# Attention's value product in groups of four query tiles, in a hybrid encoder block

## The chip, the cores and the metric

The kernel runs on one core of one Trainium2 chip. The metric is the device time of one execution in microseconds (us), as the median of several runs. Before the change that is 3035.97 us over 3 runs, from 3034.92 to 3040.51.

## The reference

One encoder block over 2048 positions of width 1024, all in f32. Cut to what matters here:

```python
proj = rms_norm(h, ln_mix_g) @ w_in                  # one combined input projection
y_a  = mlstm_group(...)                              # 4 heads x 128, chunks of 128, both directions
# y_b: 4 heads of attention over all 2048 keys
sc = einsum('bqhd,bkhd->bhqk', q_nope, k_nope) + einsum('bqhr,bkr->bhqk', q_rope, k_rope)
pr = softmax(sc * scale, axis=-1)
y_b = einsum('bhqk,bkhd->bqhd', pr, v)
h = h + concatenate([y_a, y_b], -1) @ w_out
h = h + conv_gated_mlp(rms_norm(h, ln_ffn_g), ...)   # up 1024 -> 2 x 2816, conv of 3, gate, down
h = h + sigmoid(rms_norm(h, ple_norm_g) @ w_ple_gate) * rms_norm(p @ w_ple_proj, ple_post_g)
out = rms_norm(h, final_g)
```

## The kernel before

All large products are made three times: each f32 operand is split into a high and a low part (`split`: ScalarE casts the high part, L114, VectorE subtracts to get the low one, L117), and `mm3` (L125) multiplies low by high, high by low and high by high into the same PSUM bank. The stages follow each other: `in_proj`, `attend` with the mLSTM as side work, `out_proj`, `up`, `down` with the last part, `ple`. Buffers in SBUF are places with fixed names: x0 to x15, w0 to w13, t0 to t7, s0 to s2 and u0 to u2; who writes a place waits for its last readers. Instructions of an engine stand in one order, which a scheduler makes at build time from the order in the source; in the last part of `in_proj` PE's order is the written one. Tiles named in a profile row stand without their numbers (pt, pe, bk).

**In the input projection** the columns "rest" (gates, latent queries, keys and rope part) come first. `turn_rest` (L273) transposes each 128 rows into PSUM, copies them to `rt` in place t6 (L278) and stores them (L279). The query and key columns of the mLSTM come last, 8 blocks of 128 columns (L376), while the side work `absorb`, `gates` and `q_up` is pumped.

**Attention** (`attend`, L827) makes 64 rounds, head after head, one per query tile of 128 rows. Keys and values are the same latent for all heads. A round is written as a list of steps:

```python
order = "s0 E1 . s1 E2 . . t0 . s2 . E3 . t1 . s3 . . X e0 t2 . . t3 V . .".split()
```

- s0 to s3 (`score_bank`, L846): the next tile's scores against 512 keys each, five products into one of four PSUM banks, then the row maximum on VectorE (L857).
- X (`soft`, L866): the maximum over the four banks and its scaling (L868, L869, tile nm).
- e0, and E1 to E3 in the following round (`expo`, L872): the exponentials from PSUM into pe on ScalarE with their row sums (L875). A score bank is free for the tile after once its exponential has been read. E3 is followed by the reciprocal of the row sum, into `rsums`.
- t0 to t3 (`transp`, L883): four transposes each of the current tile's probabilities into PSUM (L889, tile tb) and a split into pt, which holds two query tiles, 256 columns.
- V (`pv`, L892): half of the product of the values with pt of two query tiles, 24 matmuls of 256 columns into one bank (ppv); both halves take two rounds, so that every round has one. After the second, the reciprocals are transposed to rows (L908), copied (L910), multiplied onto the product (L911) and stored in `y_d`.
- each dot lets `pump` take some 0.73 steps of the side work, the mLSTM (L689), whose matmuls share one PSUM bank (ml, tile mb).

Tile 0's scores, maxima and exponentials come ahead of the first round (L931 to L939), behind the projection's last block.

**The output projection** (`out_proj`, L1031) loads y for 128 rows (`load_y`, L1012), splits it, multiplies it by w_out (eight splits `wo`, in x0 to x7, four of them made within attention), adds x, stores h1 and normalises (`norm_load`, L981; the scaling is L987). The last tile's transposes come at the head of `up` (`turn`, L1274). `sums` (L1109) makes differences of blocks of the normalised rows and stores them in `t_d`; `load_op` (L1129) loads and splits them for `up`. `down` (L1351) loads its weights as it goes (`load_w`, L1369).

Of the kernel before, what the change touches and what calls it, by code (L numbers as in the profile page):

```python
# [18 lines left out]
P = 128  # L19
# [17 lines left out]
SIDE = 610  # L37
# [22 lines left out]
class Block:  # L60
# [4 lines left out]
    def __init__(self, ctx, tc, d):  # L65
# [20 lines left out]
        self.vv_d = dt([P, NT, P], F32, name="vv_d")  # L86
        self.wo_d = dt([NH, P, D], F32, name="wo_d")
# [90 lines left out]
    def in_proj(self):  # L178
# [94 lines left out]
        def turn_rest(st, nn):  # L273
            pt = self.ppv.tile([P, 4, P], F32, name="rtp", tag="pv")
            for j in range(4):
                nc.tensor.transpose(pt[:, j, :], nn[:, j * P:(j + 1) * P], self.ident)
            rt = self.at("t6", [P, 4, P], name="rt")
            nc.scalar.copy(rt, pt)  # L278
            nc.sync.dma_start(self.rest_d[:, :, st * P:(st + 1) * P], rt)  # L279
# [59 lines left out]
        side, due = chain(self.absorb(), self.gates(), self.q_up()), 0.0  # L339
# [16 lines left out]
        def pump(due):  # L356
            due += 1.17
            while due >= 1:
                next(side, None)
                due -= 1  # L360
            return due

        def conv(j, u, c):
            t = self.at(next(trot), [P, 512], name="ct")
            uu, o = u[c // 2], (c % 2) * 512
# [7 lines left out]

        with self.tc.manual_schedule(engines={mybir.EngineType.PE}):
            nxt = load_qk(0)
            for j in range(8):  # L376
                ws = nxt
                if j < 7:
                    nxt = load_qk(j + 1)
                else:  # L380
                    kr = self.load_kr()
                    kv = [self.load_kv(i, w) for i, w in enumerate(("w8", "w13", "w9", "w12"))]
                u = [self.at(next(urot), [P, H + 2], name="u") for _ in range(2)]
                nc.vector.memset(u[0][:, 0:1], 0.0)
                nc.vector.memset(u[1][:, H + 1:H + 2], 0.0)
                order = range(4) if j < 7 else (3, 2, 1, 0)
                for c in order:
                    ps = self.bank()
                    for kt in range(KT):
                        f, k = divmod(kt, 4)  # L390
                        self.mm3(ps, ws[f][:, k, 0], ws[f][:, k, 1], xh[c][f][:, k, :], xl[c][f][:, k, :],
                                 kt == 0, kt == KT - 1)
                        if kt % 2 and kt < KT - 1:
                            due = pump(due)
                    o = (c % 2) * 512
                    nc.vector.tensor_tensor(u[c // 2][:, 1 + o:513 + o], ps, rrow[c // 2][:, o:o + 512], op=ALU.mult)
                    if c == 1:
                        nc.vector.tensor_copy(u[1][:, 0:1], u[0][:, H:H + 1])
                    if c == 2:
                        nc.vector.tensor_copy(u[0][:, H + 1:H + 2], u[1][:, 1:2])  # L400
                    due = pump(due)
                    if c != order[0] and (j < 7 or c > 0):
                        conv(j, u, c - 1 if j < 7 else c + 1)
                    if j == 7 and c == 3:
                        self.split_kr(kr)
                    if j == 7 and c == 2:
                        for _ in self.split_kv(kv, range(2)):
                            pass
                if j < 7:
                    conv(j, u, 3)  # L410
        for _ in side:
            pass

        def tail():
            for c in (1, 0):
                conv(7, u, c)
                yield
            yield from pause(4)
            yield from self.split_kv(kv, range(2, 4))
# [30 lines left out]
    def split_kv(self, raws, quarters):  # L450
        for i in quarters:
# [8 lines left out]
            for e in range(2):  # L460
                sl = slice((i % 2) * 1024 + e * 512, (i % 2) * 1024 + e * 512 + 512)
                self.split(raws[i][:, e * 512:e * 512 + 512], hi[:, sl], lo[:, sl])
                yield
# [225 lines left out]
    def mlstm(self):  # L689
# [38 lines left out]
        for c in range(NT - 1, 0, -1):  # L728
            kT = self.at(f"w{5 + c % 2}", [P, NH, P], name="kTb")
            nc.sync.dma_start(kT, self.qk_d[c, :, 4:8, :])  # L730
            v1 = load_v(c)
# [95 lines left out]
    def attend(self, side):  # L827
        nc = self.nc
        mm = nc.tensor.matmul
        prot, ptrot = _rot("w", (0, 1, 2)), _rot("x", (8, 9, 4, 5, 6, 7))  # L830
        kh, kl, qv = self.kh, self.kl, {}
        self.wo = []
# [39 lines left out]
        def expo(s, kb):  # L872
# [5 lines left out]
            if kb == 3:  # L878
                ri = rsums[:, s.h * NT + s.qt:s.h * NT + s.qt + 1]
                nc.vector.tensor_reduce(ri, s.rs, axis=AX.X, op=ALU.add)  # L880
                nc.vector.reciprocal(ri, ri)

        def transp(s, kb, pts):  # L883
# [6 lines left out]
            self.split(t, pts[kb][:, 0, :, o:o + P], pts[kb][:, 1, :, o:o + P])  # L890

        def pv(w, half):  # L892
            h, pr, pts = w.h, w.pr, w.pts
            if half == 0:
                w.ps = self.ppv.tile([P, 256], F32, name="ppv", tag="pv")
            vh, vl = self.vh, self.vl
            for kb in (2 * half, 2 * half + 1):
                for j in range(4):
                    kt = kb * 4 + j
                    ks = slice(kt * P, (kt + 1) * P)  # L900
                    self.mm3(w.ps, vh[:, ks], vl[:, ks], pts[kb][:, 0, j, :], pts[kb][:, 1, j, :],
                             kt == 0, kt == NT - 1)
            if half == 1:

                pb = self.tbank([P, 2, P])
                for i in range(2):
                    k = h * NT + 2 * pr + i
                    nc.tensor.transpose(pb[:, i, :], rsums[:, k:k + 1].broadcast_to([P, P]), self.ident)  # L908
                rb = self.at(f"s{pr % 3}", [P, 2, P], name="ya")
                nc.scalar.copy(rb, pb)  # L910
                nc.vector.tensor_tensor(rb, rb, w.ps.rearrange("p (a t) -> p a t", a=2), op=ALU.mult)  # L911
                for i in range(2):
                    nc.sync.dma_start(self.y_d[2 * pr + i, :, 4 + h, :], rb[:, i])
# [4 lines left out]
        order = "s0 E1 . s1 E2 . . t0 . s2 . E3 . t1 . s3 . . X e0 t2 . . t3 V . .".split()  # L918
        first = [o for o in order if o[0] == 'e']
        rate = SIDE / (len(seq) * order.count("."))  # L920
# [10 lines left out]
        load_q(0, 0)  # L931
        split_q(0, 0)
        load_q(0, 1)
        cur = start(*seq[0])
        for kb in range(4):
            score_bank(cur, kb)
        soft(cur)
        for o in first:
            expo(cur, int(o[1]))  # L939
        pts, pend = [], None  # L940
        for i, (h, qt) in enumerate(seq):
            if h == NH - 1 and qt in (4, 6, 8, 10):
                self.load_wo(qt // 2 - 2)
# [7 lines left out]
            if nxt is None:  # L951
                self.ps0 = self.pml.tile([P, 512], F32, name="wo0", tag="ml")
                self.out_mm(self.ps0, self.y0, range(4), slice(0, 512))
            for op in order:
# [10 lines left out]
                elif op[0] == "E":  # L965
                    expo(cur, int(op[1]))
                elif op == "V" and qt % 2:
                    pend = Tile()
                    pend.h, pend.pr, pend.pts = h, qt // 2, pts
                    pv(pend, 0)  # L970
                elif op == "V" and pend is not None:
                    pv(pend, 1)
            if qt % 2:
                pts = []
            cur = nxt
        pv(pend, 1)
# [27 lines left out]
    def load_wo(self, k):  # L1004
        nc = self.nc
        raw = self.at("w13" if k < 4 else ("w13", "w12")[k % 2], [P, D], name="wor")
# [24 lines left out]
    def out_proj(self):  # L1031
# [7 lines left out]
        for k in range(4, KT):  # L1039
# [4 lines left out]
        self.orot = _rot("t", (4, 5)), _rot("t", range(6))  # L1044
        sums, b11 = self.sums(0), self.load_op(0, "B11")
        for c in range(NT):
# [6 lines left out]
            if 9 <= c < 13:  # L1053
                next(sums)
                next(b11)
            if c in (13, 14):
                for _ in self.load_op(0, f"T{c - 12}"):
                    pass
# [5 lines left out]
            for hf in range(2):  # L1064
# [3 lines left out]
                self.out_mm(ps, y, range(4 if begun else 0, KT), fs)  # L1068
# [40 lines left out]
    def sums(self, b):  # L1109

        nc = self.nc
        t0 = b * 2 * SB
        for k in range(4):
# [6 lines left out]
            tt = nc.vector.tensor_tensor  # L1120
            tt(b12, b12, b11, op=ALU.subtract)
            tt(b22, b22, b12, op=ALU.subtract)
            tt(b11, b22, b11, op=ALU.subtract)
            tt(b21, b21, b22, op=ALU.subtract)
            for i, t in enumerate((b12, b22, b11, b21)):
                nc.sync.dma_start(self.t_d[b, i, :, k], t)
            yield

    def load_op(self, b, n):  # L1129

        hi, lo = [self.at(f"x{x}", [P, 4, SB], F32R, f"op{e}") for x, e in zip(self.OPX[n], "hl")]
        if b:
            self.xop[n] = hi, lo
        else:
            self.__dict__.setdefault("xop", {})[n] = hi, lo
        rot = self.orot[b or n != "B11"]
# [414 lines left out]
```

## Time and profile before

| what | value |
|---|---|
| median of 3 runs | 3035.97 us |
| the profiled execution's own time | 3039.24 us |
| its span, first to last instruction | 3037.5 us |
| mean granted clock of TensorE | 0.996 |
| PE busy | 2979.3 us, 98% |
| VectorE (DVE) busy | 1891.2 us, 62% |
| ScalarE (ACT) busy | 1358.1 us, 45% |
| DMA | 431.06 MB, mean 142 GB/s |

How to read it: the page has shares of busy time, then groups of instructions: source line, engine, operation, tile written <- tiles read, shape, count, then busy us and mean ns of one, then the idle time of the engine just ahead of them and what ended most of it. In the timeline a row has the start in us, the time it took, the engine and line, and in brackets the idle time of its engine ahead of it with what ended that. Matmuls are pipelined: the time between two starts is shorter than the duration of one, and a PE that is busy need not be at its peak. A window's row has its length, then the busy time and count of each engine, the granted clock, and the DMA's share and rate.

### The profile page before, as it was taken

Reading aid. Unit: us, or ns where it says so; the run is one execution under the profiler, and the core shown is the slowest. Engines: PE = TensorE matmul, PEld = TensorE weight load, DVE = VectorE, ACT = ScalarE, POOL = GpSimd, SP = SyncE. Lnnn points to the kernel's source line nnn. Section 1 sums busy time; section 2 is a strip of 40 time slices with the busy share of each in tenths; the row PEclk is TensorE's granted clock in tenths of the full one; section 3 lists DMA queues with packets and bytes.
Section 4 is the critical chain, followed back from the end, with each engine's and each line's share of the span. In section 5 each row is a group of like instructions: output and inputs, shape, how many; then the busy total and the mean of one; then the engine's idle time right before and its main releaser. Section 6 shows DMA issues by size and latency. Waiting matters only on the chain. (4 is left out here: it accounts for less than half of the span.)

```text
span 3037.5 us, 40758 instructions
## 1 busy us (share of the span) xinstructions
PE 2979.3 (98%) x15184; PEld 2517.3 (83%) x15184; DVE 1891.2 (62%) x3457; ACT 1358.1 (45%) x2598; POOL 141.5 (5%) x262
## 2 busy tenths in 40 slices
PE   8999999999999999999999999999999999999998
PEld 7888788888898898888778887788887888888887
DVE  7321756777777777635788888777777343334565
ACT  7211545555566565523544445444444332223444
POOL 3100000000000000000000000000000000000111
PEclk9999999999999999999999999999999999999999
DMA  6522446443333232558764335433337465444221
GB/s 190 112 70 91 124 124 190 126 146 104 101 96 93 93 98 97 171 187 303 228 210 139 132 134 198 139 125 125 124 122 229 160 221 200 146 159 148 78 79 63
DMA packets 323383, 431.06 MB, mean 142 GB/s; under 512 B 24992, under 2 KB 218480, under 8 KB 323184
## 3 DMA queue, kind: packets, MB, share of 16 engines
q1 hardware_dynamic: 323184, 428.46, 43.6%
q8 instruction: 119, 1.95, 0.3%
q14 instruction: 80, 0.66, 0.1%
HBM read 291.12 MB, written 137.26 MB: 141 GB/s over the span
## 5 line engine op out<-in xcount | busy, mean ns | idle before, releaser
L127 PE MATMUL facc<-fw,hid 128*128 128x512 f32 x2112 | 480.7, 389 | 3.9 <-ACT fw L114 2.7
L127 PEld LDWEIGHTS facc<-fw,hid 128*128 128x128 f32 x2112 | 396.2, 188 | 87.7 <-ACT fw L114 3.1
L127 PE MATMUL fxy<-oph,fw 128*128 128x512 f32 x1408 | 451.7, 394 | 6.4 <-DVE ug L1307 5.0
L127 PEld LDWEIGHTS fxy<-oph,fw 128*128 128x128 f32 x1408 | 265.7, 189 | 75.8 <-DVE ug L1307 11.5
L117 DVE TENSOR_TENSOR fw<-fwr,fw 128x1024 fp32r<-128x1024 f32 x176 | 215.3, 1223 | 165.1 <-ACT fw L114 165.1
L114 ACT CAST fw<-fwr 128x1024 fp32r<-128x1024 f32 x176 | 184.4, 1048 | 256.0 <-PE facc L127 131.6
L127 PE MATMUL fxy<-opl,fw 128*128 128x512 f32 x704 | 276.1, 392 | 0.0
L114 ACT CAST pt<-tb 128x512 fp32r<-128x512 f32 x256 | 146.9, 586 | 211.3 <-PE tb L889 210.4
L127 PE MATMUL bk<-wsp,xh 128*128 128x512 f32 (+1 forms) x768 | 235.6, 388 | 0.2 <-DVE wsp L123 0.2
L127 PE MATMUL fzs<-oph,fw 128*128 128x512 f32 x704 | 234.2, 389 | 0.0
L127 PE MATMUL ppv<-pt,kv 128*128 128x256 f32 x1536 | 203.7, 287 | 0.0
L117 DVE TENSOR_TENSOR pt<-tb,pt 128x512 fp32r<-128x512 f32 x256 | 174.0, 686 | 40.0 <-ACT pt L114 38.7
L857 DVE TENSOR_REDUCE mx<-bk 128x1 f32<-128x512 f32 x256 | 175.3, 685 | 35.8 <-PE bk L856 34.9
L127 PEld LDWEIGHTS ppv<-pt,kv 128*128 128x128 f32 x1536 | 188.9, 191 | 0.0
L875 ACT ACTIVATE pe<-bk,nm 128x512 f32<-128x512 f32 x256 | 173.9, 694 | 25.5 <-DVE nm L869 24.4
L127 PE MATMUL pgp<-pw,x3s 128*128 128x512 f32 (+1 forms) x792 | 178.7, 385 | 0.0
L127 PE MATMUL bk<-wo,yhl 128*128 128x512 f32 x744 | 174.4, 392 | 0.0
L127 PE MATMUL bk<-xh,wqk 128*128 128x512 f32 x512 | 168.1, 394 | 0.0
L127 PEld LDWEIGHTS pgp<-pw,x3s 128*128 128x128 f32 x792 | 144.5, 188 | 28.2
L127 PEld LDWEIGHTS bk<-wsp,xh 128*128 128x128 f32 x768 | 145.6, 190 | 26.5 <-DVE wsp L123 1.2
L127 PEld LDWEIGHTS bk<-wo,yhl 128*128 128x128 f32 x744 | 138.3, 188 | 28.2
L127 PE MATMUL bk<-wsp,xl 128*128 128x512 f32 (+1 forms) x384 | 150.5, 392 | 7.7 <-ACT wsp L122 7.4
(317 smaller groups left out, 5374.6 us busy)
## 6 DMA issues: line engine op xcount, KB each, us to landing
fwr<-in_w_down SPq DMA_DIRECT2D x88, 512.0 KB, 4.0
fwr<-in_w_up SPq DMA_DIRECT2D x66, 512.0 KB, 4.1
s_d<-fwr SPq DMA_DIRECT2D x44, 512.0 KB, 3.2
fws<-s_d SPq DMA_DIRECT2D x44, 512.0 KB, 3.6
hraw<-hid_d SPq DMA_DIRECT2D x33, 512.0 KB, 4.2
rw<-row_d SPq DMA_DIRECT2D x32, 512.0 KB, 5.1
hid_d<-fgv SPq DMA_DIRECT2D x22, 512.0 KB, 3.7
hid_d<-fgv SPq DMA_DIRECT2D x22, 511.5 KB, 5.1
```

Source lines behind the costliest of these rows:

```text
L114: nc.scalar.copy(hi, src)
L117: (sub or nc.vector).tensor_tensor(lo, src, _f(hi), op=ALU.subtract)
L127: mm = lambda *a, **k: self.nc.tensor.matmul(*a, **k, skip_group_check=more)
L857: nc.vector.tensor_reduce(s.mx[:, kb:kb + 1], ps, axis=AX.X, op=ALU.max)
L875: nc.scalar.activation(s.pe[:, kb % 2], s.banks[kb], AF.Exp, bias=s.nm, scale=ASCALE, accum_out=s.rs[:, kb:kb + 1])
```

## The change

The probabilities of four query tiles now form one group: pt is two tiles of 512 columns (high and low), in ten places of which a group takes eight. The product has 512 columns and takes four steps V, one for each 512 keys: two in the round that ends a group (`fourth`) and two in the next (`after`); the two rounds between (`plain`) have none, and more dots. The reciprocals of the row sums are no longer transposed for each pair: they are turned once for half of the tiles, stored in `ri_d`, and `load_y` multiplies by them. Attention begins inside the projection (`attend_begin`): the scores, maxima and exponentials of tile 0 stand among the last four blocks of matmuls, two of which go to other PSUM banks. `rt` has two places. Two output weights, not four, are split within attention. The differences of `sums` are split straight from SBUF where they had been stored and loaded again, and two weights of `down` are loaded ahead of the last steps of `up`.

```diff
-            rt = self.at("t6", [P, 4, P], name="rt")
+            rt = self.at(f"u{st % 2}", [P, 4, P], name="rt")
...
-            due += 1.17
...
+            due[0] += 1.26
...
+            att = self.attend_begin()
+            next(att)
+            vals = [self.load_kv(2 + i, w) for i, w in enumerate(("w5", "w7"))]
+            block(6, 0, self.bank)
+            conv(6, 1)
+            conv(6, 0)
+            next(att)
+            block(7, 1, self.gbank)
+            conv(7, 2)
+            next(att)
+            block(7, 0, self.gbank)
+            conv(7, 1)
+            conv(7, 0)
...
+        ptrot = _rot("x", (8, 9, 4, 5, 6, 7, 0, 1, 2, 3))
+        lastrot = _rot("x", range(2, 10))
...
         def transp(s, kb, pts):
-            o = (s.qt % 2) * P
-            if s.qt % 2 == 0:
-                pts.append(self.at(next(ptrot), [P, 2, 4, 256], F32R, "pt"))
+            o = (s.qt % 4) * P
+            if o == 0:
+                rot = lastrot if s.h == NH - 1 and s.qt == NT - 4 else ptrot
+                pts.append([self.at(next(rot), [P, 4, 512], F32R, f"pt{e}") for e in "hl"])
             t = self.tbank()
             for j in range(4):
                 nc.tensor.transpose(t[:, j, :], s.p[kb][:, j * P:(j + 1) * P], self.ident)
-            self.split(t, pts[kb][:, 0, :, o:o + P], pts[kb][:, 1, :, o:o + P])
...
+            self.split(t, pts[kb][0][:, :, o:o + P], pts[kb][1][:, :, o:o + P])
+
+        def pv(w):
+
+            kb = w.kb
+            w.kb += 1
+            if kb == 0:
+                w.ps = self.ppv.tile([P, 512], F32, name="ppv", tag="pv")
             vh, vl = self.vh, self.vl
-            for kb in (2 * half, 2 * half + 1):
...
+            for j in range(4):
+                kt = kb * 4 + j
+                ks = slice(kt * P, (kt + 1) * P)
+                self.mm3(w.ps, vh[:, ks], vl[:, ks], w.pts[kb][0][:, j, :], w.pts[kb][1][:, j, :], kt == 0, kt == NT - 1)
+            if kb == 3:
+                ya = self.at(f"u{w.g % 2}", [P, 4, P], name="ya")
+                nc.scalar.copy(ya, w.ps.rearrange("p (a t) -> p a t", a=4))
+                for i in range(4):
+                    nc.sync.dma_start(self.y_d[4 * w.g + i, :, 4 + w.h, :], ya[:, i])
...
-        order = "s0 E1 . s1 E2 . . t0 . s2 . E3 . t1 . s3 . . X e0 t2 . . t3 V . .".split()
...
+        plain = "s0 E1 . . s1 E2 . . . t0 . . s2 . E3 . . t1 . s3 . . X e0 . t2 . . t3 . .".split()
+        fourth = "s0 E1 . s1 E2 . t0 . s2 . E3 t1 V . s3 . X e0 t2 . V t3 .".split()
+        after = "s0 E1 . s1 E2 V t0 . s2 . E3 . t1 . s3 . X e0 V t2 . t3 .".split()
+        orders = after, plain, plain, fourth
+        rate = SIDE / (len(seq) // 4 * sum(o.count(".") for o in orders))
...
+        def sums(half):
+
+            pt = self.tbank([NH * 8, P])
+            nc.tensor.transpose(pt, rsums[:, half * NH * 8:(half + 1) * NH * 8], self.ident)
+            o = self.at("u2", [NH * 8, P], name="ri")
+            nc.scalar.copy(o, pt)
+            nc.sync.dma_start(self.ri_d[half * 8:half * 8 + 8].rearrange("c h t -> (c h) t"), o)
...
         yr = self.at(f"w{5 + c % 2}", [P, 8, P], name="yr")
         self.nc.sync.dma_start(yr, self.y_d[c])
+        rb = self.row_bcast(self.at(f"u{c % 2}", [P, 512], name="rb"), self.ri_d[c].rearrange("h t -> (h t)"), 512)
+        ya = yr[:, 4:8].rearrange("p h t -> p (h t)")
+        self.nc.vector.tensor_tensor(ya, ya, rb, op=ALU.mult)
...
-        for k in range(4, KT):
+        for k in range(2, KT):
             self.load_wo(k)
...
+            if not b:
+                put("T1", b12)
+                put("T2", b22)
...
+        self.wdown = self.down_weights()
+        self.wd0 = [self.wdown(c) for c in range(2)]
         rest(prev)
         conv(prev)
```

More of the change, by code (lines that the diff above doesn't have):

```diff
@@ L372, in conv @@
                               t.rearrange("p (c t) -> p c t", t=P))
+        us, wqk = {}, {0: load_qk(0)}
         with self.tc.manual_schedule(engines={mybir.EngineType.PE}):
[L375 to L410, printed above, removed]
@@ L411, in in_proj @@
-        for _ in side:
-            pass
+            for j in range(6):
+                wqk[j + 1] = load_qk(j + 1)
+                for c in range(4):
+                    block(j, c, self.bank)
+                    if c:
+                        conv(j, c - 1)
+                conv(j, 3)
+            block(6, 3, self.bank)
+            wqk[7] = load_qk(7)
+            block(6, 2, self.bank)
+            for _ in side:
+                pass
+            kr = self.load_kr()
+            keys = [self.load_kv(i, w) for i, w in enumerate(("w8", "w13"))]
@@ new lines, in in_proj @@
+            block(7, 3, self.bank)
+            conv(6, 3)
+            self.split_kr(kr)
+            block(7, 2, self.bank)
+            self.split_kv(keys, range(2))
+            block(6, 1, self.bank)
+            conv(6, 2)
+            conv(7, 3)
+            att = self.attend_begin()
[5 more added lines that the diff above has]
+            next(att)
@@ L878, in expo, with attend @@
             if kb == 3:
[L879 removed]
+                ri = rsums[:, s.qt * NH + s.h:s.qt * NH + s.h + 1]
                 nc.vector.tensor_reduce(ri, s.rs, axis=AX.X, op=ALU.add)
                 nc.vector.reciprocal(ri, ri)
+        self.steps = load_q, split_q, score_bank, start, soft, expo
+        load_q(0, 0)
+        load_q(0, 1)
+        split_q(0, 0)
+        yield
+        self.first = cur = start(0, 0)
+        for kb in range(4):
+            score_bank(cur, kb)
+        soft(cur)
+        for kb in range(2):
+            expo(cur, kb)
+        yield
+        for kb in range(2, 4):
+            expo(cur, kb)
+        yield
+    def attend(self, side):
+        nc = self.nc
+        mm = nc.tensor.matmul
+        load_q, split_q, score_bank, start, soft, expo = self.steps
+        rsums = self.gt.rearrange("p a b -> p (a b)")
+        ptrot = _rot("x", (8, 9, 4, 5, 6, 7, 0, 1, 2, 3))
+        lastrot = _rot("x", range(2, 10))
+        class Tile:
+            pass
         def transp(s, kb, pts):
[L884 to L886 removed]
+            o = (s.qt % 4) * P
+            if o == 0:
+                rot = lastrot if s.h == NH - 1 and s.qt == NT - 4 else ptrot
+                pts.append([self.at(next(rot), [P, 4, 512], F32R, f"pt{e}") for e in "hl"])
             t = self.tbank()
@@ L929, in attend @@
         rsums = self.gt.rearrange("p a b -> p (a b)")
[L931 to L939, printed above, removed]
+        def sums(half):
[4 more added lines that the diff above has]
+            nc.sync.dma_start(self.ri_d[half * 8:half * 8 + 8].rearrange("c h t -> (c h) t"), o)
+        cur, self.wo = self.first, []
         pts, pend = [], None
         for i, (h, qt) in enumerate(seq):
-            if h == NH - 1 and qt in (4, 6, 8, 10):
-                self.load_wo(qt // 2 - 2)
+            if h == NH - 1 and qt in (10, 12):
+                self.load_wo(qt // 2 - 5)
+            if h == NH - 1 and qt == 9:
+                sums(0)
             if i == len(seq) - 2:
@@ L952, in attend @@
                 self.ps0 = self.pml.tile([P, 512], F32, name="wo0", tag="ml")
-                self.out_mm(self.ps0, self.y0, range(4), slice(0, 512))
-            for op in order:
+                self.out_mm(self.ps0, self.y0, range(2), slice(0, 512))
+            for op in orders[qt % 4]:
                 if op == ".":
@@ L1054, in out_proj @@
                 next(sums)
[L1055 to L1058, printed above, removed]
             if c == 12:
@@ L1120, in sums @@
             tt = nc.vector.tensor_tensor
+            put = lambda n, t: self.split(t, self.xop[n][0][:, k], self.xop[n][1][:, k])
+            if not b:
+                put("B11", b11)
             tt(b12, b12, b11, op=ALU.subtract)
```

149 lines of the change are left out of this document (77 added, 72 removed).

## The prediction

> **What bounds the kernel now.** I read the page's busy shares first, then busy time by stage, then the groups, then the timeline around each gap of TensorE (PE), and last the granted clock. In the page each row is engine, busy us, share, count; in the stage row (a window within attention) come PE, weight loads (PEld), VectorE (DVE), ScalarE (ACT), GpSimd, clock share, DMA share and GB/s.
>
> ```profile
> span 3037.5 us, 40758 instructions
> PE 2979.3 (98%) x15184; PEld 2517.3 (83%) x15184; DVE 1891.2 (62%) x3457; ACT 1358.1 (45%) x2598; POOL 141.5 (5%) x262
> 560.00:660.00 100.00, 100.00 (x693) 91.26 (x692) 73.60 (x184) 54.86 (x133) 0.00 (x0) 1.00 0.44 135
> ```
>
> PE is never idle in that window while DVE has a quarter free. So time is won by giving PE less to do or by closing its few gaps, and lost by anything that makes PE wait. Attention is 64 rounds, one per head and query tile. A round makes the four score banks of the next tile (s0 to s3), transposes the four probability blocks of the current one (t0 to t3), and takes steps of the side work (mLSTM). The first row below, from the view by tile, has duration min/median/max and first and last start: 64 blocks of the product between 548.7 and 1264.4 us make rounds of some 11.4 us.
>
> ```profile
> L127 PE MATMUL ppv<-pt,kv x1536: 277/283/367, 548.7 to 1264.4; 128*128 128x256 f32 x192
> L127 PE MATMUL ppv<-pt,kv 128*128 128x256 f32 x1536 | 203.7, 287 | 0.0
> L114 ACT CAST pt<-tb 128x512 fp32r<-128x512 f32 x256 | 146.9, 586 | 211.3 <-PE tb L889 210.4
> L117 DVE TENSOR_TENSOR pt<-tb,pt 128x512 fp32r<-128x512 f32 x256 | 174.0, 686 | 40.0 <-ACT pt L114 38.7
> L857 DVE TENSOR_REDUCE mx<-bk 128x1 f32<-128x512 f32 x256 | 175.3, 685 | 35.8 <-PE bk L856 34.9
> L908 PE MATMUL tb<-ident,gt 128*128 128x128 f32 x64 | 12.1, 270 | 0.0
> ```
>
> **The value product.** A mean duration of a matmul includes the pipeline's drain, so its price is read from start to start. Before, the timeline has 24 products of 256 columns in one block; a run of 48 with 512 columns stands in the output projection.
>
> ```profile
> 901.17 0.60 PE L889 MATMUL tb<-ident,pe 128*128 128x128 f32 x4
> 901.53 3.11 PE L127 MATMUL ppv<-pt,kv 128*128 128x256 f32 x24
> 901.81 0.59 ACT L114 CAST pt<-tb 128x512 fp32r<-128x512 f32 x1 [0.74 <-PE tb L889]
> 903.31 0.68 ACT L875 ACTIVATE pe<-bk,nm 128x512 f32<-128x512 f32 x1
> 904.48 0.38 PE L908 MATMUL tb<-ident,gt 128*128 128x128 f32 x2
> 904.61 0.48 PE L852 MATMUL bk<-kv,q_t 128*128 128x512 f32 x1
> 1425.59 11.15 PE L127 MATMUL bk<-wo,yhl 128*128 128x512 f32 x48
> L127 PE MATMUL bk<-wo,yhl 128*128 128x512 f32 x744 | 174.4, 392 | 0.0
> ```
>
> The old block holds PE from 901.53 to 904.48: 2.95 us. A new one is 12 products; the run of 48 gives (11.15 - 0.39) / 47 = 0.229 each (0.39 is the mean duration of one, which its last takes alone), so 2.75, or 2.83 if each block pays the slow first product that 48 share. Both kernels have 64 blocks: between 64 x 0.20 = 12.8 and 64 x 0.12 = 7.7 us less. I take **-10**. The Trainium skill (TensorE: Matmul & The Clock Gate, section Back-to-back issue gap) gives a gap of columns / 2.4 GHz plus about 2.5 ns: by it joining two products saves only the 2.5 ns, 768 times, some 2 us (an estimate from that page), and the sum would be 8 us higher. The trace's two rows speak for more than that.
>
> The 64 transposes of L908, with their ScalarE copy and VectorE product, go. Four transposes take 0.60 with a drain of 0.27 (L908's mean), so (0.60 - 0.27) / 3 = 0.11 each: **-7**. The scaling moves to `load_y`, 16 DVE products of 512 columns in the output projection, where this engine waits for PE between its operations (3.05 us in the row below): nothing, and 16 x 0.69 = 11 us were that cover gone.
>
> ```profile
> 1425.00 0.69 DVE L1069 TENSOR_TENSOR xt<-xt,bk 128x512 f32<-128x512 f32 x1 [3.05 <-PE bk L127]
> ```
>
> **What the product hid.** Score bank s0 of a tile reuses the PSUM bank that the exponential e0 of the tile before reads. In the rows at 901 us, t3 is followed by the product, and its 2.95 us cover the cast of t3, e0 and its wait: s0 starts at 904.61 with no idle time. Only the first rounds of attention have no product yet, and there the same chain is bare:
>
> ```profile
> 538.15 0.66 PE L889 MATMUL tb<-ident,pe 128*128 128x128 f32 x4 [1.13 <-DVE pt L117]
> 538.84 0.58 ACT L114 CAST pt<-tb 128x512 fp32r<-128x512 f32 x1 [1.15 <-PE tb L889]
> 539.32 0.41 ACT L114 CAST q_t<-q_t 128x256 fp32r<-128x256 f32 x1
> 540.07 0.14 DVE L869 TENSOR_SCALAR nm<-nm 128x1 f32<-128x1 f32 x1
> 540.30 0.69 ACT L875 ACTIVATE pe<-bk,nm 128x512 f32<-128x512 f32 x1 [0.57 <-DVE nm L869]
> 541.13 0.50 PE L852 MATMUL bk<-kv,q_t 128*128 128x512 f32 x1 [2.33 <-ACT pe L875]
> ```
>
> PE idles 2.33 us. In the changed kernel the product stands in two rounds of four, with all four blocks; the two `plain` rounds have none. The built order has, after a plain round, t3 and at most a few mLSTM products on PE ahead of the next s0, and on ACT the cast of t3 ahead of e0. The chain by the rows: 0.69 from t3's first transpose to its cast (538.15 to 538.84), 0.48 until ACT's next operation (to 539.32), 0.83 from e0 to s0 (540.30 to 541.13), 2.00 together; PE fills 0.44 of it with the transposes: 1.56 bare. I set this against the built order at all 63 boundaries, taking the later of this route and that over the last score bank (maximum 0.69, two small steps, and whatever DVE has between them), plus any ACT work queued ahead of e0, less the PE work in between, with 0.23 for a pair of mLSTM products:
>
> ```profile
> 907.45 0.39 PE L792 MATMUL mb<-v,mk 128*128 128x129 f32 x2
> 907.68 0.39 PE L793 MATMUL mb<-cf,qi 128*128 128x129 f32 x2
> ```
>
> For the kernel before, only the first two boundaries come out bare, 2.3 and 2.0 us, as the trace has it (its gaps at 523 to 529 and at 541). For the changed one 32 do: the s0 behind every plain round, and that of the third tile, which has no product ahead of it yet. They are 2.8, 1.2, 1.7, 1.4, 0.9, 1.6, 1.1, 0.9, 0.2, 1.6, 2.7, 0.8, 1.0, 1.6, 1.6, 0.9, 0.2, 0.2, 1.4, 0.2, 1.1, 1.7, 1.3, 1.1, 1.6, 0.2, 1.9, 1.6, 1.1, 0.9, 0.2, 1.6: **+38.6**, between 28 (mLSTM work slides into a third of them) and 50 (the chain as slow as at 541, 0.4 more at each).
>
> **Two side effects.** A plain round takes 18 of a group's 52 side steps, 13 before. DVE, 73.6% of an 11.4 us round or 8.4 us, has 8 x 0.69 = 5.5 us of maxima and subtractions; the other 2.9 grow by 18/13 to 4.0, together 9.5. PE's round before is 20 score products (20 x 0.229 = 4.6), 16 transposes (1.8), the product (2.95), L908 (0.2) and so 1.9 of side work; a plain round has 4.6 + 1.8 + 1.9 x 18/13 = 9.0. DVE is then as full as PE, and waits of up to 0.5 us in each of 32 plain rounds are possible: 0 to 16. I take **+3**, near the lower end because the bare waits above give DVE time to catch up. And the clock:
>
> ```profile
> 998.88 0.50 PE L852 MATMUL bk<-kv,q_t 128*128 128x512 f32 x1 [1.83 <-ACT pe L875]
> 999.75:1003.16 3.41, 3.41 (x11) 2.73 (x10) 1.66 (x5) 2.52 (x13) 0.72 (x2) 0.50 0.14 41
> 1546.48 0.50 PE L127 MATMUL fxy<-oph,fw 128*128 128x512 f32 x1 [1.75 <-DVE ug L1307]
> 1542.46:1549.29 6.83, 5.08 (x23) 3.85 (x22) 6.83 (x9) 2.27 (x3) 0.00 (x0) 1.00 0.79 250
> ```
>
> An idle time of 1.83 us was followed by 3.41 us at clock 0.50, 1.7 us of work lost; one of 1.75 us was not. Two or three of my 32 exceed 1.83: **+3.4**, up to 15 if the nine of 1.6 and more do it. The Trainium skill (same page, Part 1, The HAM clock gate) has the clock halved after an idle window of about 3.4 us; by that none of these waits would do it and the sum is 3.4 lower; the 1.83 us row speaks against it.
>
> **What the change closes.** Attention now begins inside the projection: the scores and exponentials of tile 0 lie under 48 matmuls of the last two blocks.
>
> ```profile
> 526.21 0.71 PE L716 MATMUL mb<-v,kk 128*128 128x129 f32 x4 [2.44 <-DVE nm L869]
> 528.34 0.92 PE L716 MATMUL mb<-v,kk 128*128 128x129 f32 x4 [1.42 <-DVE cb L720]
> 528.71:532.13 3.42, 3.42 (x12) 2.74 (x11) 1.95 (x7) 1.67 (x6) 0.00 (x0) 0.50 0.60 176
> 542.37:545.78 3.41, 3.41 (x11) 2.72 (x10) 1.92 (x5) 1.79 (x5) 0.00 (x0) 0.50 0.00 1
> 105.14 0.58 ACT L278 COPY rt<-rtp 128x512 f32<-128x512 f32 x1 [12.05 <-DMA rest_d<-rt]
> 105.78 1.11 PE L276 MATMUL rtp<-ident,nn 128*128 128x128 f32 x4 [3.74 <-ACT rt L278]
> 105.46:108.87 3.41, 3.09 (x10) 2.81 (x11) 1.27 (x8) 2.09 (x7) 1.14 (x3) 0.50 0.27 77
> 1459.96 1.11 PE L1274 MATMUL fzs<-ident,xt 128*128 128x128 f32 x4 [5.09 <-DVE xt L987]
> ```
>
> The idle 2.44, 1.42, 1.13 and 2.33 and two half-clock windows, 7.3 + 3.4 = **-10.7**, go; what stays bare there (2.8, 1.2, 1.7) is in the 38.6. The store buffer `rt` becomes two: the copy no longer waits 12.05 us for the store before it, PE's 3.74 and 1.7 of clock go, **-5** (0 if the slow store only stalls a later copy). The 5.09 us at the head of the up projection I leave at nothing: the built order has the same seven splits ahead of the normalisation. So also the two weights loaded before the down projection: ACT still has their casts behind the same two. The last product's tiles lie where six output weights must be split, under 8 us of product: nothing, up to +4.
>
> Sum: -10 - 7 + 38.6 + 3 + 3.4 - 10.7 - 5 = **+12.3**. The profiled execution took 3039.24 us around its span of 3037.5, 3.3 over the median of the three runs, 3035.97; so 3051.5 for such an execution, **3048** for a median.
>
> **Rivals.** (1) *The chain stays covered*: ACT has 45% free in the window above, and if the casts come early enough the waits shrink to a fourth, 10 us. For it: before, PE waited nowhere in the steady rounds for more than the 1.83 us. Against: ACT takes its queue in order, and e0 stands behind a cast that needs t3. -10 - 7 + 10 - 10.7 - 5: 23 less, 3013, faster. The point that decides is a mean of 0.8 us per bare boundary (26 us in all). (2) *The waits feed the clock*: 15 for the clock and 12 for DVE instead of 3.4 and 3, and waits of 50 instead of 38.6, put it 44 above the time before, 3080. For it: the row at 541; against: most waits are under 1.7. (3) *Even*: waits of 28 and an undisturbed clock leave -10 - 7 + 28 + 3 - 10.7 - 5 = -2, 3034. (4) The change does less than it says, 512 columns costing as much a column as 256: 10 more than forecast, 3058, inside the forecast's case.
>
> **How the numbers follow.** 0.2% (6 us) is what a measurement can tell here. Forecast, 3042 to 3062: 0.42. Beyond it, by rival 2: 0.18. Even, 3030 to 3042: 0.16. Rival 1: 0.24. So faster 0.24, same 0.16, slower 0.60. The range from 3014 to 3074 leaves out about a tenth at each end, half of rival 1 and half of rival 2.
>
> **What would show it.** Right: product blocks of 2.8 us, no L908; s0's first matmul idle by about 40 us in all behind ACT's exponential, in two rounds of four; DVE above 85% in plain rounds; no gap over 3 us at 102 and little at 520 us; the 5 us before the up projection still there. Wrong: s0 idle under 20 us, or more than six half-clock windows within attention.

## The result and the profile after

The changed kernel takes 3091.65 us (median of 4 runs, 3088.72 to 3094.45), the kernel before beside it 3035.85: a ratio of 1.018, 95% interval 1.0165 to 1.0195. It is 56 us slower; forecast were 12, and 3048. The direction was right, the size not. First the head of the page after and, from the windows, attention from the first score product to the last product with the values: the row of before, then that of after (columns: length, then busy us and count of PE, weight loads, VectorE, ScalarE, GpSimd, clock, DMA share, GB/s).

```profile
span 3087.2 us, 38996 instructions
PE 2987.8 (97%) x14354; PEld 2473.6 (80%) x14354; DVE 1890.6 (61%) x3441; ACT 1358.9 (44%) x2586; POOL 142.4 (5%) x262
```
```profile
518.60:1264.40 745.80, 728.15 (x4929) 655.97 (x4928) 546.82 (x1410) 439.90 (x1194) 46.05 (x64) 0.99 0.35 109
```
```profile
511.40:1311.30 799.90, 745.23 (x4139) 622.55 (x4138) 541.95 (x1391) 444.35 (x1188) 45.70 (x64) 0.98 0.33 103
```

PE has 830 matmuls fewer and is busy 8.5 us longer; its idle time in attention (length less busy) rose from 17.6 to 54.7 us. By stretch, from the starts in both traces:

| stretch | before | after | difference |
|---|---|---|---|
| start to first s0 | 518.6 | 511.4 | -7.2 (10.9 us of projection, 48 matmuls x 0.227, moved behind s0: so +3.7) |
| attention | 745.7 | 799.9 | +54.2 (less the 10.9: +43.3) |
| to the first transposes of the up projection | 195.6 | 200.9 | +5.3 (2.7 of it, 12 x 0.23, are products with w_out that the kernel before makes ahead of its last product with the values) |
| up | 842.2 | 840.2 | -2.0 |
| down | 735.3 | 734.9 | -0.4 |

A second split of attention needs no modelled ends. For each matmul I take the time to the next start. Its usual time is the median of its shape in that trace, halved windows left out; what it takes above that is its excess (below it, the excess is negative). Excess at a "boundary", the end of a round, lies between a tile's last score product and the next tile's first.

| attention, us | before | after |
|---|---|---|
| usual times summed | 716.3 | 709.9 (with the 10.9) |
| excess at the ends of the rounds after / plain / plain / fourth | 8.7, 1.9, 1.1, 6.5 | 1.6, 28.0, 31.5, -1.2 |
| excess inside the rounds | 6.7 | 16.0 |
| excess in windows of halved clock | 4.5 | 14.1 |

The work did get cheaper: 716.3 + 10.9 - 709.9 = 17 us less, of which 2.7 only moved behind attention; the rest is the product and the transposes of the sums. The ends of the two plain rounds took 59.5 us more than their work where the same rounds had 3.0. The five longest groups of waits of PE (line waited for: us, times, longest), in attention of the changed kernel:

```profile
PE bk L878 <- ACT pe L901: 28.3, 25, 3.2
PE mb L847 <- DVE hy L842: 5.4, 4, 3.2
PE tb L944 <- DVE ptl L118: 4.4, 8, 0.9
PE mb L737 <- DVE cf L741: 3.2, 5, 1.1
PE mb L818 <- ACT hy L828: 2.2, 3, 1.3
```

Only half is s0 (L878) behind the exponential; the rest stands mostly ahead of the mLSTM's matmuls (mb). The timeline shows why, at the end of a second plain round (start, time taken, engine and line; brackets: idle time before, and what ended it):

```profile
747.40 0.39 PE L882 MATMUL bk<-kv,q_t 128*128 128x512 f32 x1
747.63 1.03 PE L944 MATMUL tb<-ident,pe 128*128 128x128 f32 x8
747.90 0.68 DVE L883 TENSOR_REDUCE mx<-bk 128x1 f32<-128x512 f32 x1
748.57 0.67 DVE L800 TENSOR_TENSOR qi<-qk,rw 128x512 f32<-128x512 f32 x1
749.16 0.60 DVE L830 SCALAR_TENSOR_TENSOR hy<-mb,den,hy 128x128 f32<-128x128 f32 x2
749.53 1.28 ACT L799 ACTIVATE mk<-mk,cols 128x128 f32<-128x128 f32 x4
749.68 0.14 DVE L894 TENSOR_REDUCE nm<-mx 128x1 f32<-128x4 f32 x1
749.75 0.67 DVE L118 TENSOR_TENSOR ptl<-tb,pth 128x512 fp32r<-128x512 f32 x1
749.90 0.69 PE L737 MATMUL mb<-v,kk 128*128 128x129 f32 x4 [1.24 <-DVE nm L894]
750.34 0.13 DVE L895 TENSOR_SCALAR nm<-nm 128x1 f32<-128x1 f32 x1
750.71 0.40 ACT L115 CAST q_t<-q_t 128x256 fp32r<-128x256 f32 x1
751.01 0.68 ACT L901 ACTIVATE pe<-bk,nm 128x512 f32<-128x512 f32 x1
751.84 0.60 PE L878 MATMUL bk<-kv,q_t 128*128 128x512 f32 x1 [1.25 <-ACT pe L901]
```

The last maximum is done at 748.58. Then VectorE makes 1.1 us of mLSTM work, nm's first step, a subtraction for t3, nm's second; ScalarE puts four mLSTM operations (749.53) and the cast of a query tile ahead of e0; s0 starts at 751.84. PE's mLSTM matmuls of 0.69 us stand in this gap, but had to wait 1.24 us first. PE is idle for 2.49 us in all, and the window behind has half the clock (the 0.50 in the second row):

```profile
748.68:752.09 3.41, 0.94 (x5) 0.78 (x6) 3.25 (x10) 3.41 (x11) 0.00 (x0) 1.00 0.97 265
752.09:755.50 3.41, 3.41 (x9) 2.62 (x9) 0.92 (x3) 2.86 (x14) 0.38 (x2) 0.50 0.40 153
```

### The profile page after: what moved, and what is told of

The parts are those of the page before. It is cut to its first block, busy times and chain, and to the rows that moved or that the text cites. A ratio compares the mean times of both kernels' runs of the same rounds, so it can differ in the third digit from the quotient of the medians.

```text
span 3087.2 us, 38996 instructions
## 1 busy us (share of the span) xinstructions
PE 2987.8 (97%) x14354; PEld 2473.6 (80%) x14354; DVE 1890.6 (61%) x3441; ACT 1358.9 (44%) x2586; POOL 142.4 (5%) x262
## 3 DMA queue, kind: packets, MB, share of 16 engines
q8 instruction: 113, 1.85, 0.2%
## 5 line engine op out<-in xcount | busy, mean ns | idle before, releaser
L115 ACT CAST pth<-tb 128x512 fp32r<-128x512 f32 x256 | 147.2, 589 | 232.2 <-PE tb L944 230.9
L118 DVE TENSOR_TENSOR ptl<-tb,pth 128x512 fp32r<-128x512 f32 x256 | 173.7, 685 | 86.0 <-ACT pth L115 82.5
L128 PE MATMUL ppv<-pth,kv 128*128 128x512 f32 x512 | 171.8, 397 | 0.0
L128 PEld LDWEIGHTS pgp<-pw,x3s 128*128 128x128 f32 x792 | 144.4, 188 | 28.3
L128 PE MATMUL bk<-xh,wqk 128*128 128x512 f32 x480 | 159.0, 397 | 0.0
L944 PE MATMUL tb<-ident,pe 128*128 128x128 f32 x1024 | 154.5, 276 | 4.4 <-DVE ptl L118 4.4
```

What stands on the lines that cost most here:

```text
L115: nc.scalar.copy(hi, src)
L118: (sub or nc.vector).tensor_tensor(lo, src, _f(hi), op=ALU.subtract)
L128: mm = lambda *a, **k: self.nc.tensor.matmul(*a, **k, skip_group_check=more)
L944: nc.tensor.transpose(t[:, j, :], s.p[kb][:, j * P:(j + 1) * P], self.ident)
```

## The experiments

They ran on three other chips (e1 to e4, e5 to e8, e9 to e12), on each of which the kernel before takes 3047 us instead of 3036; so they are compared by their ratio to it, which for the changed kernel there is 1.0171 (e10, on the third of them). The times in the expectations are on the first scale. Idle times and losses of the clock are from one execution of each kernel: for the changed kernel the halved clock cost 15.4 us of attention in the first trace and 20.5 in e10 (half the length of the windows at 0.50), so a difference of 5 us in it says nothing.

**e1, the product back in pairs.** The old `transp`, `pv` and order of a round; the copy of the product without the sums' transposes; all else as changed.

```diff
...
-        orders = after, plain, plain, fourth
+        order = "s0 E1 . s1 E2 . . t0 . s2 . E3 . t1 . s3 . . X e0 t2 . . t3 V . .".split()
...
```

> The product goes back to pairs of query tiles (256 columns, half of the key blocks in every round, the old order of a round); every other edit of the change stays, the sums' transposes are still gone. Theory (the rounds without product cost it: bare waits before s0, the side work's waits, the halved clock, some 66 us in attention, against 10 for the 512 columns): attention from first s0 to last product about 740 us instead of 800, the whole 3031, under the kernel before. Rival (the other edits cost most of it: the start moved into the projection, the late output weights, the scaling moved out): attention stays above 775, the whole 3060 or more.

Ratio 0.9971 (0.9958 to 0.9984), attention 744.5 us. Its waits in attention, to set beside the 28.3 and 4.4 above:

```profile
PE bk L878 <- ACT pe L901: 6.8, 4, 3.0
PE tb L943 <- DVE pt L118: 4.2, 12, 1.0
```

The grouping with its order of rounds costs the whole loss: 2% of the time is between the two. The rival (the other edits) falls.

**e2, three boundaries of four covered.**

```diff
...
-        after = "s0 E1 . s1 E2 V t0 . s2 . E3 . t1 . s3 . X e0 V t2 . t3 .".split()
-        orders = after, plain, plain, fourth
+        after = "s0 E1 . s1 E2 . t0 . s2 . E3 . t1 . s3 . X e0 V t2 . t3 .".split()
+        first = "s0 E1 . . s1 E2 . . t0 . s2 . E3 . t1 . s3 . . X e0 V t2 . . t3 .".split()
+        orders = after, first, plain, fourth
```

> One product block is moved out of the round behind the fourth into the first plain round, so that three of a group's four boundaries have a block ahead of s0 and 16 instead of 32 are bare. Theory (bare boundaries): half of the 28 us of s0 waits, half of the side waits and of the halved clock go, 25 to 33 less than the changed kernel, 3060 to 3067. Rival (the squeeze of side steps and VectorE in the plain rounds): only the rounds that no longer are plain gain, 10 to 15 less, 3078. Rival (the other edits): within 5 of 3092.

Ratio 1.006 (1.0043 to 1.0076), 34 us under the changed kernel, a little more than expected. The excess at the end of the first plain round fell from 28.0 (e10) to 1.8, that of the second is still 27.9; the clock's loss in attention is 11.9, against 20.5 in e10. Each bare boundary costs for itself. The edit also takes the side steps of the round that gets the block from 18 to 13; e7 shows that this alone leaves its end bare (26.8).

**e3, t1 behind e0 in the plain rounds.**

```diff
-        plain = "s0 E1 . . s1 E2 . . . t0 . . s2 . E3 . . t1 . s3 . . X e0 . t2 . . t3 . .".split()
+        plain = "s0 E1 . . s1 E2 . . . t0 . s2 . E3 . . s3 . . X e0 . t1 . . t2 . . t3 . .".split()
```

> In the two plain rounds the second transposition block t1 moves from ahead of s3 to behind e0, with a side step; the blocks of the product stay. Theory (the chain from e0 to s0 is bare because PE runs out of work): 0.45 to 0.7 us of cover at each of 32 boundaries, 14 to 20 us less wait, and fewer halved windows, 3068 to 3077. Rival (the rounds are full on VectorE, so that a wait only moves elsewhere): 3092 within 6.

Ratio 1.0094 (1.0078 to 1.011): 23 us less than e10, at the upper end of what was expected. PE's idle time in attention is 39.9 instead of 58.8, the clock's loss 8.5 instead of 20.5.

**e4, filling the gap with work for nobody.**

```diff
+            if qt % 4 in (1, 2) and nxt:
+                fl = self.ppv.tile([P, 512], F32, name="fill", tag="pv")
+                for f in range(8):
+                    j = (f % 4) * P
+                    nc.tensor.transpose(fl[:, j:j + P], cur.p[3][:, j:j + P], self.ident)
```

> Eight transposes of the last probability block, into a bank that nobody reads, are added behind t3 of each plain round: 32 x 8 x 0.11 = 28 us more of work on PE, in the place of the bare waits (28 us of s0 waits, mean 0.9). If the waits are idle time that anything could fill and they are also what halves the clock: no more time for the work, fewer windows at 0.50, 3077 to 3092. If the rounds are limited by something else on PE or the waits have moved: 3110 to 3120. If the clock is halved by something other than these waits: nine or so windows stay within attention.

Ratio 1.0179 (1.0164 to 1.0194), the same as without. The 256 transposes took 28 us of PE (256 x 0.11) and cost nothing that can be measured: idle time fell from 58.8 to 38.7 and the clock's loss from 20.5 to 11.9. PE was waiting, not short of time. Some of the waits are longer than the fill.

**e5 and e6, no side work in the rounds.**

```diff
-        self.attend(chain(tail, self.mlstm()))
+        for _ in chain(tail, self.mlstm()):
+            pass
+        self.attend(iter(()))
```

> The kernel before with the whole side work (mLSTM) run ahead of attention, so that a round is only scores, transposes and product. It is the ground for the next run: by the dense prices 20 x 0.229 + 16 x 0.11 + 2.95 + 0.2 = 9.5 us a round, attention from first s0 to last product 608 us if PE is never idle, up to 620 with the start. Both theories expect this.

> The changed kernel with the side work ahead of attention in the same way. Dense: 586 us (a plain round 6.4, one with two blocks 11.9). Theory (the chain from the last score bank through the maximum, e0 and the cast to s0 is bare by itself): 1.5 to 1.9 us at each of the 32 boundaries with nothing of the side work there, attention 634 to 647 us. Rival (what is lost at a boundary is mostly the side work's own waits, whose matmuls stand ahead of s0 and wait for VectorE and for their one bank): under 0.8 us each, attention under 612, less than the kernel before in this form.

Each has one execution. Tile 0 still stands ahead of the side work, so the lengths from s0 that I expected can't be read; the rounds can (tiles 4 to 60). The kernel before has 9.38 us in every round, the expected price, and PE never waits there. The changed one has 11.83 (after), 8.51 and 8.50 (plain) and 11.90 (fourth), mean 10.19. So without any side work the grouping costs 0.81 us a round, about as with it (11.47 to 12.27, 0.80; 0.95 from e9 to e10). At the ends of the plain rounds the excess is 32.6 + 23.5 = 56.1 us (2.05 at each first one, 1.57 at each second), where the changed kernel has 59.5. The one group of waits that PE has there in 590 us, and a boundary of each kind, the second plain round first:

```profile
PE bk L880 <- ACT pe L903: 45.5, 28, 2.2
```
```profile
1116.63 0.39 PE L884 MATMUL bk<-kv,q_t 128*128 128x512 f32 x1
1116.86 1.05 PE L946 MATMUL tb<-ident,pe 128*128 128x128 f32 x8
1117.12 0.68 DVE L885 TENSOR_REDUCE mx<-bk 128x1 f32<-128x512 f32 x1
1117.49 1.07 ACT L115 CAST pth<-tb 128x512 fp32r<-128x512 f32 x2 [1.01 <-PE tb L946]
1118.03 0.15 DVE L897 TENSOR_SCALAR nm<-nm 128x1 f32<-128x1 f32 x1
1118.45 0.70 ACT L903 ACTIVATE pe<-bk,nm 128x512 f32<-128x512 f32 x1
1119.30 0.50 PE L880 MATMUL bk<-kv,q_t 128*128 128x512 f32 x1 [1.39 <-ACT pe L903]
```
```profile
1109.27 0.16 DVE L896 TENSOR_REDUCE nm<-mx 128x1 f32<-128x4 f32 x1
1109.55 0.69 DVE L118 TENSOR_TENSOR ptl<-tb,pth 128x512 fp32r<-128x512 f32 x1
1110.16 0.14 DVE L897 TENSOR_SCALAR nm<-nm 128x1 f32<-128x1 f32 x1
1110.39 0.69 ACT L903 ACTIVATE pe<-bk,nm 128x512 f32<-128x512 f32 x1 [0.39 <-DVE nm L897]
1111.23 0.50 PE L880 MATMUL bk<-kv,q_t 128*128 128x512 f32 x1 [1.88 <-ACT pe L903]
```

The chain is bare by itself: at the first, e0 waits for the two casts; at the other a subtraction stands between nm's two steps, and s0 comes 0.5 later. The rival (the side work's own waits) falls as a cause of the bare boundaries. But the side work undoes its own cover. With it, 9.4 mLSTM matmuls stand on average in each of the 31 boundaries behind plain rounds, some 1.1 us at 0.23 a pair. Yet from the last score product to e0 the changed kernel takes 3.20 us on average, e6 2.07: the maximum is ready 0.5 us later, nm another 0.5, and e0 0.1, behind the mLSTM's work on VectorE and ScalarE. And s0 follows e0 within 0.9 us at 26 of the 31 (at all 31 in e6), so it is this chain that ends last.

**e7, side steps even.** 13 dots in every round.

```diff
+        plain = "s0 E1 . s1 E2 . . t0 . s2 . E3 . t1 . s3 . . X e0 t2 . . t3 . .".split()
+        fourth = "s0 E1 . s1 E2 . . t0 . s2 . E3 . t1 V . s3 . . X e0 t2 . V . t3 . .".split()
+        after = "s0 E1 . s1 E2 V . t0 . s2 . . E3 . t1 . s3 . . X e0 V t2 . . t3 . .".split()
```

> The changed kernel with the side steps even over the rounds, 13 each, where the plain rounds took 18 and the rounds with product 8. Theory (the bare chain): the same bare boundaries with about one mLSTM matmul fewer in each, no gain, within 8 us of the changed kernel's ratio of 1.018. Rival (the squeeze: 18 side steps fill VectorE in a plain round, and the side work's waits stand ahead of s0): 15 to 25 us less, a ratio of 1.010 to 1.013.

Ratio 1.0111 (1.0089 to 1.0134): the rival's range. Of the 19 us by which attention is shorter than in e10 (807.5 to 788.3), 10.3 are clock and 7.5 idle time. At the ends of the plain rounds PE still idles 41.8 us, instead of 47.4: they stay bare. The squeeze was real, then, though it acts more through the clock than through the length of the waits.

**e8, e2 and e3 together**: e2's rounds, and in the remaining plain round

```diff
...
+        plain = "s0 E1 . . s1 E2 . . t0 . . s2 . . E3 . . s3 . X e0 t1 . t2 . t3".split()
...
```

> One product block in the first plain round as in the second run, and in the remaining plain round t1 moved behind e0. If both cures add up: the 18 us over the kernel before of the second run, less half of the 25 us that the shift brought at twice as many boundaries: 5 to 7 us over it, a ratio of 1.002. If what is left is the side work's waits, the shift brings nothing more here: 1.006.

Ratio 1.0033 (1.002 to 1.0047), between the two expectations. Idle time in attention fell from e2's 36.8 to 27.9. The end of the plain round still has 24.1 us of excess. This round also goes from 18 side steps to 13, so e7's cure has a share in the gain, which wasn't separated.

**e9 and e10, both kernels unchanged, on the chip of e11 and e12.**

> The kernel before, for a profile on the chip of the runs e1 to e8, where its time is 3047 us instead of 3036. If the 11 us are a fixed difference of that chip, every stage is longer by its share or the transfers at the start are; if they are one of the waits that the change takes away (the store buffer at 102 us, the head of the up projection), that wait is longer here, and the experiments look better against the kernel before than they are.

> The changed kernel on this chip, as ground for the experiments. If the ratio to the kernel before is the same: 1.017 to 1.020, about 3102 us, and the even side steps of e7 bring 15 to 20. If the changed kernel does not have what makes the kernel before slower here: 3091 us, a ratio of 1.014, and e7 brings 8.

e9: 3047.53 (one execution), its profile 8.3 us longer than on the first chip: 2.3 ahead of s0 (the store buffer's wait is 5.6 instead of 3.74), 5.3 in up. e10: ratio 1.0171 (1.0154 to 1.0187), as on the first chip. Its attention took 807.5, 7.6 more than there; the halved clock has 5.1 of it.

**e11, e1 with the old rate of side work in the projection.**

```diff
-            due[0] += 1.26
+            due[0] += 1.17
```

> e1 (pairs, 256 columns, all else changed) with the side work of the projection pumped at 1.17 as before, not 1.26. If the gap of 2.9 us ahead of the gates' product at 333 us and the halved window behind it come from the faster pump: 4 us less than e1, a ratio of 0.9958. If the gap is in the new order of the blocks: as e1, 0.997.

Ratio 0.9967 (0.9955 to 0.9979): 3 us less than e1 in the medians, which the intervals don't separate. The wait that the changed kernel had gained at 333 us (first row) is nearly gone (second, e11), but two of 1.8 and 1.5 us are new there at 484 and 488 us:

```profile
PE gps L665 <- DVE mg L661: 2.9, 1, 2.9
```
```profile
PE gps L665 <- DVE mg L661: 0.6, 1, 0.6
```

**e12, the kernel before with four small edits**: the sums turned once and multiplied in `load_y`, `rt` in two places, the differences split from SBUF, two weights of `down` early.

```diff
-            rt = self.at("t6", [P, 4, P], name="rt")
+            rt = self.at(f"u{st % 2}", [P, 4, P], name="rt")
...
-                nc.scalar.copy(rb, pb)
-                nc.vector.tensor_tensor(rb, rb, w.ps.rearrange("p (a t) -> p a t", a=2), op=ALU.mult)
+                nc.scalar.copy(rb, w.ps.rearrange("p (a t) -> p a t", a=2))
...
```

> The kernel before with four of the change's edits alone: the sums turned once and multiplied in the output projection, two places for rt, the differences split from SBUF, two weights of down loaded early. The product, the order of a round, the pump and the start of attention are as before. If my terms hold: -7 for the transposes, -5 for rt, -4 for the head of the up projection: 16 less, a ratio of 0.995. If the start within the projection is what e1 gained by: 0.997 to 0.998.

Ratio 0.9952 (0.994 to 0.9963), 3032.88 us: the fastest of all, faster than the kernel before and the changed one. From the last product to the up projection it takes 192.3 us, e11 200.8.

## Why the prediction was right or wrong

- **Product, -10: right.** A block, from its first start to the next matmul, has a median of 2.82 us instead of 2.96 (64 x 0.13 = 8.5 us), without side work 2.79 instead of 2.96 (e6, e5: 10.7); the 2 us by the Trainium skill (TensorE: Matmul & The Clock Gate, Back-to-back issue gap) would have been too little. **Transposes of the sums, -7: right** (attention 745.4 us in e9, 739.3 in e12).
- **Bare waits, +38.6: mechanism and places right, size wrong; here most of the error lies.** Without side work the chain was sized well: in e6 t3's transposes start at 1117.30 (1116.86 + 4 x 0.11) and s0 at 1119.30, the forecast's 2.00; at the ends of the first plain rounds it is 0.5 more, for the subtraction between nm's two steps. It stood bare at the ends of the plain rounds, as said. What failed is the step "less the PE work in between, with 0.23 for a pair of mLSTM products": the boundaries cost 59.5 us, no less than with no mLSTM there (56.1). The mLSTM's PE work was taken off, but its VectorE and ScalarE work lies ahead of nm and e0, as in the rows from 748.57 to 749.53, and makes the chain longer by as much (3.20 for 2.07 us up to e0, against 1.1 us of matmuls).
- **Squeeze, +3: too small.** VectorE's load was right: 9.5 and 9.3 us in a plain round, 88% and 79% of it. But the excess inside the rounds rose by 9.3, and evening out the side steps (e7) brought 18 us of the ratio, over half of it clock.
- **Clock, +3.4: wrong; its loss in attention rose from 5.1 to 15.4** (20.5 in e10). The step was to count single waits over 1.83 us. It is the idle time within one window of 3.41 us that counts: at 748 two waits of 1.24 and 1.25 made it, in other places 0.70 and 1.40. Rival 2 had this one right, and its 3080 was the nearest of the cases. Nine half-clock windows within attention are also more than the six that the forecast named as a sign of being wrong. (Its list, as printed, has twelve waits of 1.6 and more, not nine: 20 us at its own price.)
- **Attention's start, -10.7: wrong.** Its waits changed places: 0.54, 2.12, 0.61 and 0.94 us and 6.83 us at half clock still lie between 532 and 549 us. Start and attention together take 1255.2 us in e11, with the new start, and 1257.2 in e12, with the old one; the 2 us are no gain, since 12 products with w_out (2.7 us) stand behind them in e11.
- **rt, -5: mostly right, -3.5.** The last transposition into rtp starts at 121.9 us instead of 125.4; a wait of 1.0 us is new at 111. But the side work's faster rate, for which I had no term, made the wait at 333 us 2.9 instead of 0.6, with a halved window in the first trace; PE's idle time ahead of s0 rose from 16.2 to 19.6. Where the 3.74 stood, the transposes of the changed kernel have no wait:

```profile
102.32 0.60 PE L277 MATMUL rtp<-ident,nn 128*128 128x128 f32 x4
107.79 0.60 PE L277 MATMUL rtp<-ident,nn 128*128 128x128 f32 x4
```

- **Head of up, nothing: too careful**, 5.09 became 1.1, and 6.83 us at half clock from 1457 us on went with it. **Output weights late, nothing, up to +4: too small**; e11 takes 8.5 us longer there than e12, 5.8 without the 12 products that moved. The waits of the changed kernel at both places:

```profile
PE fzs L1336 <- DVE xt L1042: 1.1, 1, 1.1
```
```profile
PE bk L128 <- DVE yhl L118: 1.9, 1, 1.9
PE wo L128 <- DVE wo L118: 1.3, 2, 0.7
```

Within attention the forecast was -10 - 7 + 38.6 + 3 + 3.4 - 10.7 = +17.3 and the traces have +43.3: 26 of the 37 us (49.7 - 12.3, of the spans) by which the sum fell short. By the second table these are +56.5 at the ends of the plain rounds for 38.6, +9.6 in halved windows for nothing (3.4, less the two windows in the 10.7), +9.3 inside the rounds for 3, and -17 of work as forecast; the ends of the other rounds fell by 14.8, where 7.3 of idle time were to go. The other 11 are the pump, the late weights and what rt did not save.

## What to carry to other kernels

Work that covers a chain of dependences is worth more than its own cost: the product's blocks hid about 2 us at every tile, and merging them into fewer rounds saved some 9 us and bared 59. The 7 us of the sums' transposes needed no merging, as e12 shows. Before joining work into larger pieces, list which boundary each old piece covered, and count side work as cover only if its work on the other engines doesn't stand in the chain's own queues. Where rounds become unequal for one engine, the others' load per round becomes their bound in the short ones.

## What the runs showed of the hardware

The clock is judged in fixed windows, by the idle time of PE within each. In e6, where the waits are regular, the halved windows start at 1192.0, 1314.9, 1396.8 and 1478.7 us: multiples of 3.413 us apart (36, 24, 24). Twelve waits there took 1.87 or 1.88 us, and these four halved the clock. The first pair of rows has such a wait across the border of two windows (1.37 and 0.51 idle), the second one whole in a window:

```profile
1147.63:1151.04 3.41, 2.04 (x13) 1.50 (x12) 3.18 (x8) 1.98 (x4) 0.00 (x0) 1.00 0.00 0
1151.04:1154.45 3.41, 2.90 (x15) 2.40 (x16) 1.36 (x5) 2.47 (x8) 0.00 (x0) 1.00 0.00 0
1188.59:1192.00 3.41, 1.53 (x12) 1.12 (x11) 2.78 (x6) 2.05 (x5) 0.00 (x0) 1.00 0.00 0
1192.00:1195.41 3.41, 3.41 (x9) 2.64 (x10) 0.92 (x3) 1.82 (x6) 0.00 (x0) 0.50 0.00 0
```

The fourth row has the 0.50. No wait of 1.4 halved it there. In the changed kernel a wait of 3.17 us,

```profile
1296.13 0.50 PE L847 MATMUL mb<-ident,hy 128*128 128x128 f32 x2 [3.17 <-DVE hy L842]
```

lies across a border, 1.85 and 1.32 us, and halved nothing. The limit is not sharp: in that kernel 0.70 and 0.88 in one window (up to 840.8 us) were enough, where 1.75 (up to 1096.8) were not. A forecast should therefore add the idle time of neighbouring waits and price each window that comes out about half idle at 1.7 us, half of 3.41. The Trainium skill (TensorE: Matmul & The Clock Gate, Part 1, The HAM clock gate) speaks of an idle window of about 3.4 us: the length agrees with the spacing here, but about half of it idle was enough.
